# Two layers of a hybrid trunk: the S5 input projections on x times g, with the norm's scale put on behind them

## The chip, the core and the metric

The kernel runs on one core of one Trainium2 chip. A core has five engines, each with its own queue of instructions that it works off in order: PE multiplies matrices, DVE and ACT work on tiles, POOL and SP mostly issue transfers here. The metric is the device time of one execution in microseconds, lower is better.

## What is computed

The reference is a trunk of two layers on x of 512 positions by 1024 features, in float32. Cut to what matters:

```
def _rmsnorm(x, g):
    y = xf * lax.rsqrt(jnp.mean(xf * xf, axis=-1, keepdims=True) + RMS_EPS)
    return (y * g.astype(jnp.float32)).astype(x.dtype)
...
for i in range(DEPTH):                      # DEPTH = 2
    h = _rmsnorm(x, norm_mix_g[i])
    proj = h @ w_in[i]
    (z, xbc, dt_raw, q, k, v, qi, ki, wi, rwkv_cols, s5_u, gate_cols) = _split_last(proj, IN_SPLITS)
    ...                                     # four mixers: SSD, sparse attention, RWKV-7, S5
    x = x + (merged.astype(x.dtype) @ w_out[i]).astype(x.dtype)
    h = _rmsnorm(x, norm_ffn_g[i])
    x = x + _swiglu(h, ffn_w1[i], ffn_w3[i], ffn_w2[i]).astype(x.dtype)
return _rmsnorm(x, norm_final_g)
```

The norm divides every position by the root of its own mean square. The S5 mixer takes the 512 columns `s5_u` of the projection, and its state matrices come from small parameter tensors (`s5_a_re`, `s5_a_im`, `s5_log_dt`, `s5_b_*`, `s5_c_*`).

## The kernel before

x lies transposed, features on the partitions: eight tiles of 128 features by 512 positions. Each float32 operand of a large product is split in a rounded high part and a low part (`hh` and `hl` for h, `wh` and `wl` for weights), and a product takes three matmuls (`mm3`, L302 to L304: high by high, low by high, high by low). One projection of 128 columns (`pin`, through `proj`) is thus 8 times 3 = 24 matmuls of 128x512. Its weights come by one transfer of 512 KB on SP's queue into `raw` (two buffers); ACT rounds them to `wh` (L295), DVE subtracts to `wl` (L296). The output `pj` lies in one of two buffers in PSUM (`pp`): a projection starts only when the one two before it has been read out.

The code calls every piece of work with a class (`at("x0")`, `"w"`, `"e"`, `"m"`, `"x"`, `"u"`, in falling urgency), and a scheduler sorts the instructions of each engine by it once, at build time. On the chip nothing overtakes within an engine.

Start of layer 0. `first_stats` squares the four tiles of x as they come from memory (positions on the partitions), takes the root on ACT and scales x on DVE to `xs` (L210). `first_norm` turns `xs` by 32 transposes on PE (L221) and splits the result times g into `hh` and `hl` (L324, L325). `first_x` turns x itself by 32 more transposes (L231), copies it out (`xr`, L233) and stores it to `xd` in memory, for later. `s5_load` issues 13 transfers of S5 parameters on POOL's queue, in class `"w"`.

Start of layer 1. `norm` sums the squares over the features (`rstd`: 4 small products, L257, in 8 passes), spreads the reciprocal root over the partitions (`rep`: 4 products, L266), scales each tile to `h` (L281), rounds it (L282) and subtracts (L283).

Then, in both layers, `s5` calls four projections (u0 to u3 below) and ACT copies each from PSUM with its positions permuted (`us`, L968). In layer 0 DVE and ACT then build the S5 tables from the parameters: a chain of some 60 operations from `s5are` (L782) to `s5E` (L887), which ends in two steps for the first half of S5's groups, each followed by a group of 16 small matmuls (`s5_in`: 8 of L903, 8 of L904). In layer 1 these tables have been made during the feed-forward of layer 0. The next mixer, `dsa`, begins with a projection of 44 columns (`misc`), one for the index queries (QI) and then q, k and v. q takes the PSUM buffer that `misc` leaves when DVE has made `dskl` from it (L595).

The feed-forward's last loop runs over the eight output tiles d: 66 matmuls `pf`, then DVE adds them to x (L558), and ACT and DVE add the squares to `acc` (L249).

Of the kernel before, what the change touches and what calls it, by code (L numbers as in the profile page):

```python
# [10 lines left out]
F32 = mybir.dt.float32  # L11
# [74 lines left out]
class Trunk:  # L86
# [113 lines left out]
    def first_stats(self):  # L200
        nc = self.nc
        ss = self.sp.tile([128, 4], F32, name="ss", bufs=1)
        sr = self.sp.tile([128, 4], F32, name="sr", bufs=1)
        rr = self.sp.tile([128, 4], F32, name="rr", bufs=1)
        xs = [self.A(k, [D], f"xs{k}") for k in ("A0", "A1", "B5", "B6")]
# [5 lines left out]
        self.xs = xs  # L211

    def first_norm(self):
        nc = self.nc
        self.hh = self.cp.tile([128, KD, S], F32R, name="hh", tag="hh")
        self.hl = self.cp.tile([128, KD, S], F32R, name="hl", tag="hl")
# [8 lines left out]
    def first_x(self):  # L225
        nc = self.nc
        self.xd = self.dp.tile([D, S], F32, name="xd")
        for d in range(KD):
            ps = self.P("xrp")
            for t in range(4):  # L230
                nc.tensor.transpose(ps[:, t * 128:(t + 1) * 128], self.xt[t][:, d * 128:(d + 1) * 128], self.ident)  # L231
            x = self.T("xr")
            nc.scalar.copy(x, ps)  # L233
            self.q("xd").dma_start(self.xd[d * 128:(d + 1) * 128], x)
# [71 lines left out]
    def proj(self, pieces, M=128, act=None, mix=False):  # L306
# [8 lines left out]
    def pin(self, c0):  # L315
        return self.proj([(0, self.w_in[:, c0:c0 + 128])])
# [30 lines left out]
    def layer(self, i):  # L347
# [3 lines left out]
        if i == 0:  # L351
            with self.at("x0"):
                self.first_stats()
            with self.at("w"):
                self.s5_load(0, "B")
        with self.at("m", "Tb"):
            if i:
                self.norm("norm_mix_g")
            else:
                self.first_norm()  # L360
# [146 lines left out]
    def ffn(self):  # L507
# [1091 lines left out]
```

## Time and profile before

| | us |
|---|---|
| median of three runs | 2313.12 (2310.33 to 2317.92) |
| the profiled execution | 2318.86 |
| its span, on which all rows below count | 2317.1 |
| PE busy in the span | 2242.8 (97%) |
| DVE busy | 1448.4 (63%) |
| ACT busy | 921.0 (40%) |
| POOL busy | 103.6 (4%) |

The profile is of one execution. Rows of a timeline give the start in the span, the busy time, the engine, the line, what is written from what, how many instructions the row stands for and, in brackets, how long the engine had waited and for whom. Matmuls overlap, so that 24 of them take less than 24 times the busy time of one; from start to start is what counts.

### The profile page before, as it was taken

To read this page: it belongs to the slowest core of one execution; us is meant where nothing else is said; L and a number is where in the kernel's file an instruction comes from. 1 tells how busy PE (TensorE), PEld (TensorE's weight loads), DVE (VectorE), ACT (ScalarE), POOL (GpSimd) and SP (SyncE) were. 2 spreads that over 40 slices of the span, in tenths; PEclk is the share of its full clock that TensorE was granted. 3 is DMA by queue.
4 is the path that set the end of the run, shared out by engine and by line. 5 is a ranking of instruction groups with operands and counts; after the bars stand their busy time and mean duration, and the time that the engine had idled before them with its cause. 6 is when DMAs were issued, how large, how long until landed. Compare 5 with 4: busy or idle time off the path is not lost.

```text
span 2317.1 us, 32591 instructions
## 1 busy us (share of the span) xinstructions
PE 2242.8 (97%) x12660; PEld 1789.5 (77%) x12660; DVE 1448.4 (63%) x2676; ACT 921.0 (40%) x1455; POOL 103.6 (4%) x180
## 2 busy tenths in 40 slices
PE   6999999999999999999999999999999999999998
PEld 5777777777778888887878777687777888888786
DVE  5669867767678587543244696568668775444333
ACT  5443464244642343322233335533456333222232
POOL 3320000000000101000012000000000000000000
PEclk9999999999999999999999999999999999999999
DMA  7444552444166435433365445443333653333332
GB/s 219 114 104 128 144 170 80 116 101 124 55 205 204 119 92 166 125 97 105 111 187 150 123 124 168 123 101 105 91 110 106 222 160 91 100 97 95 89 98 86
DMA packets 429186, 290.08 MB, mean 125 GB/s; under 512 B 65024, under 2 KB 386768, under 8 KB 427432
## 3 DMA queue, kind: packets, MB, share of 16 engines
q1 hardware_dynamic: 419520, 261.45, 39.3%
q0 software_dynamic: 8512, 26.43, 4.1%
q8 instruction: 99, 1.62, 0.3%
q14 instruction: 55, 0.45, 0.1%
q10 hardware_dynamic: 1000, 0.13, 0.0%
HBM read 237.30 MB, written 51.43 MB: 125 GB/s over the span
## 4 chain that ended last, share of the span: by engine, by line
PE 81%; DVE 11%; DMA 4%; issue 2%; ACT 2%; SPq 0%; DVEq 0%; ACTq 0%; POOLq 0%
PE pj L303 16%; PE pj L304 16%; PE pj L302 16%; PE pf L304 3%; PE pf L302 3%; PE pf L303 3%; PE pb L302 3%; PE pb L303 3%; PE pb L304 3%; DVE wl L296 2%; DMA rnd<-rwrn 1%; PE lgp L656 1%; PE ptp L674 1%; PE po L679 1%; DVE score L709 1%
## 5 line engine op out<-in xcount | busy, mean ns | idle before, releaser
L302 PE MATMUL pj<-hh,wh 128*128 128x512 f32 x1888 | 750.1, 398 | 11.0 <-DVE conv L1453 4.9
L304 PE MATMUL pj<-hh,wl 128*128 128x512 f32 x1888 | 749.7, 397 | 0.4 <-DVE wl L296 0.4
L303 PE MATMUL pj<-hl,wh 128*128 128x512 f32 x1888 | 749.7, 397 | 0.1
L295 ACT CAST wh<-raw 128x1024 fp32r<-128x1024 f32 x336 | 348.6, 1037 | 922.6 <-PE pj L303 344.3
L296 DVE TENSOR_TENSOR wl<-raw,wh 128x1024 fp32r<-128x1024 f32 x336 | 405.2, 1206 | 350.8 <-ACT wh L295 348.9
L302 PEld LDWEIGHTS pj<-hh,wh 128*128 128x128 f32 x1888 | 356.3, 189 | 91.0 <-issue 8.6
L303 PEld LDWEIGHTS pj<-hl,wh 128*128 128x128 f32 x1888 | 356.4, 189 | 81.7 <-issue 9.0
L304 PEld LDWEIGHTS pj<-hh,wl 128*128 128x128 f32 x1888 | 356.0, 189 | 79.1 <-issue 6.3
L302 PE MATMUL pf<-hid,wh 128*128 128x512 f32 x352 | 137.9, 392 | 1.6 <-ACT wh L295 1.6
L304 PE MATMUL pf<-hid,wl 128*128 128x512 f32 x352 | 137.7, 392 | 0.5 <-DVE wl L296 0.5
L303 PE MATMUL pf<-hid,wh 128*128 128x512 f32 x352 | 136.9, 390 | 0.0
L302 PE MATMUL pb<-yh,wh 128*128 128x512 f32 x256 | 100.9, 394 | 0.0
L303 PE MATMUL pb<-yl,wh 128*128 128x512 f32 x256 | 100.8, 394 | 0.0
L304 PE MATMUL pb<-yh,wl 128*128 128x512 f32 x256 | 100.3, 392 | 0.0
L536 DVE TENSOR_TENSOR fa<-fa,pj 128x512 f32<-128x512 f32 x44 | 30.2, 688 | 95.3 <-PE pj L304 95.2
L533 DVE TENSOR_TENSOR fa<-pj,rb 128x512 f32<-128x512 f32 x44 | 30.4, 691 | 88.6 <-PE pj L304 88.6
L302 PEld LDWEIGHTS pf<-hid,wh 128*128 128x128 f32 x352 | 66.1, 188 | 16.8 <-ACT wh L295 3.4
L304 PEld LDWEIGHTS pf<-hid,wl 128*128 128x128 f32 x352 | 66.1, 188 | 16.0 <-DVE wl L296 2.6
L303 PEld LDWEIGHTS pf<-hid,wh 128*128 128x128 f32 x352 | 66.1, 188 | 13.4
L664 ACT ACTIVATE lg<-lg,mn 128x128 f32<-128x128 f32 (+3 forms) x64 | 35.8, 559 | 61.6 <-DVE mn L662 60.0
L302 PEld LDWEIGHTS pb<-yh,wh 128*128 128x128 f32 x256 | 48.1, 188 | 10.7 <-DVE m L476 0.7
L303 PEld LDWEIGHTS pb<-yl,wh 128*128 128x128 f32 x256 | 48.1, 188 | 9.8
(493 smaller groups left out, 2977.5 us busy)
## 6 DMA issues: line engine op xcount, KB each, us to landing
raw<-in_w_in SPq DMA_DIRECT2D x146, 512.0 KB
raw<-in_ffn_w SPq DMA_DIRECT2D x120, 512.0 KB
gates<-gate SPq DMA_DIRECT2D x64, 256.0 KB
gld<-gates SPq DMA_DIRECT2D x64, 256.0 KB
raw<-in_w_branch SPq DMA_DIRECT2D x32, 512.0 KB
raw<-in_w_out SPq DMA_DIRECT2D x16, 512.0 KB
raw<-in_ffn_w SPq DMA_DIRECT2D x16, 384.0 KB
bias<-relb POOLq DMA_DIRECT2D x16, 256.0 KB, 3.1
```

Of the source, the lines that this page charges most:

```text
L295: nc.scalar.copy(wh[:, :n], raw[:, :n])
L296: nc.vector.tensor_sub(wl[:, :n], raw[:, :n], wh[:, :n].bitcast(F32))
L302: mm(ps, wh, ah, start=first, stop=False)
L303: mm(ps, wh, al, start=False, stop=False)
L304: mm(ps, wl, ah, start=False, stop=last)
L533: nc.vector.tensor_mul(a, p1, rb)
L536: nc.vector.tensor_mul(a, a, p3)
L656: i = mm(ps[e][:, :W], q[er[e], qt * 128:(qt + 1) * 128], k[er[e], :W], start=True, stop=True)
L664: nc.scalar.activation(t[:, :W], t[:, :W], AF.Exp, scale=-1.0, bias=mn[e][:, qt:qt + 1], accum_out=sm[e][:, qt:qt + 1])
L674: nc.tensor.transpose(pp[:, b * 128:(b + 1) * 128], t[:, b * 128:(b + 1) * 128], self.ident)
L679: i = mm(po[er[e], qt * 128:(qt + 1) * 128], vt[:, b, er[e]], pt[:, e, b * 128:(b + 1) * 128], start=(b == 0), stop=(b == qt))
L709: nc.vector.match_replace(sc[:, :W], m8, sc[:, :W], PICK)
```

## The change

In both layers u0 to u3 are now projected from x times g, without the norm's factor. The factor r (one number per position) is put on when DVE reads u0 to u3 out of PSUM (`u_out`, a product with `rb`). Halfway in u1 the factor is spread over the partitions (`spread`, called as `mid`), and ACT copies it to `rb`. `rescale` then makes the h of the norm from x, g and `rb`, tile by tile, over the old `hh` and `hl`; of its eight subtractions four go to POOL. Everything from `misc` on uses these.

In layer 0 x is turned once, straight from the loaded tiles: ACT writes `hh` and half of the copies `self.x`, DVE the other half and `hl`; the stores to `xd` read `self.x`. The S5 loads wait, behind a copy of one column of the first weight tile (`late`). In layer 1 `hh` and `hl` of x times g are written inside the feed-forward's last loop, and `norm` is gone.

```diff
 def first_stats(self):
-            nc.scalar.activation(xs[t], self.xt[t], AF.Square, accum_out=ss[:, t:t + 1])
-            nc.scalar.activation(sr[:, t:t + 1], ss[:, t:t + 1], AF.Sqrt, scale=1.0 / D, bias=self.eps[:, 0:1])
-            nc.vector.reciprocal(rr[:, t:t + 1], sr[:, t:t + 1])
-            nc.vector.tensor_scalar(xs[t], self.xt[t], rr[:, t:t + 1], None, op0=OP.mult)
+            nc.scalar.activation(junk[:, t % 2], self.xt[t], AF.Square, accum_out=ss[:, t:t + 1])
+        nc.scalar.activation(sr, ss, AF.Sqrt, scale=1.0 / D, bias=self.eps[:, 0:1])
+        nc.vector.reciprocal(self.rr, sr)
...
+    def first_x(self):
         for d in range(KD):
             with self.at("x0", "TaTb"[d % 2 * 2:][:2]):
                 ps = self.P("xtp")
                 for t in range(4):
-                    nc.tensor.transpose(ps[:, t * 128:(t + 1) * 128], self.xs[t][:, d * 128:(d + 1) * 128],
+                    nc.tensor.transpose(ps[:, t * 128:(t + 1) * 128], self.xt[t][:, d * 128:(d + 1) * 128],
                                         self.ident)
-                self.split_out(self.hh[:, d], self.hl[:, d], ps, self.g0[:, d:d + 1])
+                g = self.g0[:, d:d + 1]
+                nc.scalar.activation(self.hh[:, d], ps, AF.Copy, scale=g)
+                eng = nc.vector.tensor_copy if d % 2 else nc.scalar.copy
+                eng(self.x[d], ps)
+                nc.vector.scalar_tensor_tensor(self.hl[:, d], self.x[d], g, self.hh[:, d].bitcast(F32),
+                                               op0=OP.mult, op1=OP.subtract)
...
-    def norm(self, g):
-        pr = self.rep(self.rstd(self.acc, 1.0 / D, self.eps[:, 0:1], "nrm"), "nrm")
+    def rescale(self, g, rb):
         for d in range(KD):
             h = self.T("h")
-            nc.vector.scalar_tensor_tensor(h, self.x[d], self.v(g, d), pr, op0=OP.mult, op1=OP.mult)
+            nc.vector.scalar_tensor_tensor(h, self.x[d], self.v(g, d), rb, op0=OP.mult, op1=OP.mult)
             nc.scalar.copy(self.hh[:, d], h)
-            nc.vector.tensor_sub(self.hl[:, d], h, self.hh[:, d].bitcast(F32))
+            eng = nc.gpsimd if d % 2 else nc.vector
+            eng.tensor_sub(self.hl[:, d], h, self.hh[:, d].bitcast(F32))
...
 # proj, over the 8 blocks k
+                if mid and k == KD // 2:
+                    mid()
...
 # feed-forward, last loop
                 nc.vector.tensor_add(self.x[d], self.x[d], ps)
                 if i < L - 1:
+                    self.split_out(self.hh[:, d], self.hl[:, d], self.x[d], self.v("norm_mix_g", d))
...
 def s5(self, ar):
-        for j in range(4):
-            ps = self.pin(C_U + j * 128)
-            us = self.T("us", tag="G")
-            nc.scalar.copy(us.rearrange("p (t c) -> p c t", c=64), ps.rearrange("p (c t) -> p c t", t=8))
+        def u_out(j, ps):
+            us = self.T("us", tag="G")
+            ct = lambda a: a.rearrange("p (c t) -> p c t", t=8)
+            tt(us.rearrange("p (t c) -> p c t", c=64), ct(ps), ct(rb), op=OP.mult)
...
+        pu = [self.pin(C_U)]
+        if not ahead:
+            with self.at("w"):
+                late = self.sp.tile([128, 1], F32, name="late", bufs=1)
+                self.s5_load(0, ar, after=nc.gpsimd.tensor_copy(late, self.raw[:, :1]))
+        with self.at("u"):
+            st = self.rstd(self.acc, 1.0 / D, self.eps[:, 0:1], "nrm") if ahead else self.rr
+        pu.append(self.pin(C_U + 128, spread))
+        with self.at("e"):
+            rb = self.T("rb", tag="KS")
+            nc.scalar.copy(rb, pr[0])
+        for j in range(4):
+            if j > 1:
+                pu.append(self.pin(C_U + j * 128))
+            with self.at("e"):
+                u_out(j, pu[j])
+        self.rescale("norm_mix_g", rb)
```

What this does to the sorted queues is shown at three places. The lines of the new code have moved by one or two: L301 to L303 are the three matmuls now.

PE in layer 0, at the first `s5kt` (L903), the first matmul that needs a finished `s5E` from DVE. Rows with 44 columns are `misc`, those with 128x512 QI. Before:

```order
L304 MATMUL pj<-hh,wl 44x512
L302 MATMUL pj<-hh,wh 128x512 [waits Activation_49]
L303 MATMUL pj<-hl,wh 128x512
L903 MATMUL s5kt<-s5tab_552,s5E 128x16 [waits DVE_49]
L904 MATMUL s5pt<-cst,s5E 128x128
```

After, the last rows of QI and what follows:

```order
L303 MATMUL pj<-hh,wl 128x512
L301 MATMUL pj<-hh,wh 128x512
L302 MATMUL pj<-hl,wh 128x512
L303 MATMUL pj<-hh,wl 128x512
L903 MATMUL s5kt<-s5tab_535,s5E 128x16 [waits DVE_49]
L904 MATMUL s5pt<-cst,s5E 128x128
```

Of QI two matmuls stood ahead of the first group of `s5kt`, and the second group stood between others of QI. Now all 24 stand ahead of it, both groups follow one another, and q comes behind both.

DVE in layer 0, from the second `us` on, ahead of the larger part of the S5 chain. Before, at the comparable place (L839 to L863 belong to the chain):

```order
L839 TENSOR_TENSOR s5erk<-s5erk,ere 128x32 [waits DVE_49]
L820 TENSOR_TENSOR s5t_534<-s5ami,s5are 128x32 [waits DVE_49]
L860 TENSOR_TENSOR s5tab<-s5raw,s5fr 128x512 [waits DMASW6_49,DMASW0_49]
L822 TENSOR_TENSOR s5t_534<-s5t_535,s5t_534 128x32 [waits DVE_49]
L839 TENSOR_TENSOR s5erk<-s5erk,ere 128x32
L296 TENSOR_TENSOR wl<-raw,wh 128x1024 [waits DMAHW1_49,PE_49,Activation_49]
```

After:

```order
L974 TENSOR_TENSOR us<-pj,rb 128x64x8 [waits PE_49]
L295 TENSOR_TENSOR wl<-raw,wh 128x352 [waits DMAHW5_49,DMAHW4_49,Activation_49]
L282 TENSOR_TENSOR hl<-h,hh 128x512 [waits Activation_49]
L279 SCALAR_TENSOR_TENSOR h<-x_107,cols,rb 128x512 [waits DVE_49]
L282 TENSOR_TENSOR hl<-h,hh 128x512 [waits Activation_49]
L279 SCALAR_TENSOR_TENSOR h<-x_107,cols,rb 128x512 [waits DVE_49]
L282 TENSOR_TENSOR hl<-h,hh 128x512 [waits Activation_49]
L279 SCALAR_TENSOR_TENSOR h<-x_107,cols,rb 128x512 [waits Pool_49]
L279 SCALAR_TENSOR_TENSOR h<-x_107,cols,rb 128x512 [waits DVE_49]
L974 TENSOR_TENSOR us<-pj,rb 128x64x8 [waits DMAHW6_49,PE_49]
```

All four `us`, eight `h` and DVE's four `hl` stand ahead of most of the chain; one `h` waits for POOL.

PE between the layers, from the last `pf` of the feed-forward. Before:

```order
L304 MATMUL pf<-hid,wl 128x512
L257 MATMUL nrms<-cst,acc 128x1 [waits DVE_49,PE_49]
L257 MATMUL nrms<-cst,acc 128x1 x3
L266 MATMUL nrmr<-cst,nrmst_9788 128x128 [waits DVE_49,PE_49]
L266 MATMUL nrmr<-cst,nrmst_9788 128x128 x3
L302 MATMUL pj<-hh,wh 128x512 [waits Activation_49]
```

After, the last block of u0 and the first of u1, 21 matmuls behind the last `pf`:

```order
L301 MATMUL pj<-hh,wh 128x512 [waits Activation_49]
L302 MATMUL pj<-hl,wh 128x512 [waits DVE_49]
L303 MATMUL pj<-hh,wl 128x512
L258 MATMUL nrms<-cst,acc 128x1 [waits DVE_49,PE_49]
L258 MATMUL nrms<-cst,acc 128x1 x3
L301 MATMUL pj<-hh,wh 128x512
```

The statistics' products have moved from ahead of u0 to behind it, and `nrmr` to the middle of u1.

## Rows read from the trace of the kernel before

**Rows 1.** the page, busy time of each engine, its share and instructions

```profile
PE 2242.8 (97%) x12660; PEld 1789.5 (77%) x12660; DVE 1448.4 (63%) x2676; ACT 921.0 (40%) x1455; POOL 103.6 (4%) x180
```

**Rows 2.** waits, 0 to 80 us: engine, line, released by; us, times, longest

```profile
PE pj L302 <- ACT us L968: 2.5, 1, 2.5
```

**Rows 3.** timeline of PE, layer 0: start, us, instruction, [idle before <- releaser]

```profile
20.06 0.50 PE L302 MATMUL pj<-hh,wh 128*128 128x512 f32 x1 [0.57 <-ACT hh L324]
...
63.88 0.40 PE L903 MATMUL s5kt<-s5tab,s5E 128*128 128x16 f32 x2 [1.53 <-DVE s5E L887]
...
66.51 0.63 PE L302 MATMUL pj<-hh,wh 128*128 128x512 f32 x1
...
69.50 0.59 PE L303 MATMUL pj<-hl,wh 128*128 128x512 f32 x1
...
75.79 0.40 PE L302 MATMUL pj<-hh,wh 128*128 128x512 f32 x1
```

**Rows 4.** timeline of DVE, the S5 chain of layer 0

```profile
30.81 0.19 DVE L782 COPY s5are<-s5ap 128x32 f32<-128x32 f32 x1 [3.73 <-PE s5ap L780]
...
44.46 0.19 DVE L805 TENSOR_TENSOR s5sh<-s5sh 128x32 f32<-128x32 f32 x1 [6.51 <-ACT s5sh L804]
...
62.59 1.24 DVE L887 TENSOR_TENSOR s5E<-s5E,s5tab 128x1024 f32<-128x1024 f32 x1
...
67.80 1.24 DVE L887 TENSOR_TENSOR s5E<-s5E,s5tab 128x1024 f32<-128x1024 f32 x1
```

**Rows 5.** groups by line, 0 to 80 us: ACT copies; DVE out of PSUM

```profile
L233 ACT COPY xr<-xrp 128x512 f32<-128x512 f32 x8 | 4.5, 591 | 6.9 <-DMA xd<-xr 6.9
...
L968 ACT COPY us<-pj 128x512 f32<-128x512 f32 x4 | 4.3, 1074 | 0.0
...
L322 DVE TENSOR_TENSOR dsql<-pj,dsqh 128x512 fp32r<-128x512 f32 x1 | 0.7, 683 | 0.0
```

**Rows 6.** timeline of POOL and ACT, the first 30 us

```profile
2.32 1.01 POOL L753 DMA_DIRECT2D s5raw<-in_s_a_re  x2
...
12.81 1.16 POOL L764 DMA_DIRECT2D s5raw<-in_s_c_im  x1
...
16.58 0.54 POOL L176 MEMSET sm<- 128x512 f32 x1
...
28.90 4.22 POOL L198 DMA_DIRECT2D relb<-rel  x8 [1.56 <-DMA rel<-oh]
...
9.21 1.06 ACT L207 ACTIVATE xsB<-xin 128x1024 f32<-128x1024 f32 x1 [0.18 <-DMA xin<-in_x]
...
18.37 1.04 ACT L295 CAST wh<-raw 128x1024 fp32r<-128x1024 f32 x1 [7.68 <-DMA raw<-in_w_in]
```

**Rows 7.** windows: stretch, length, busy of each engine (count), clock, DMA share, GB/s

```profile
0.00:10.00 10.00, 0.00 (x0) 0.00 (x0) 0.39 (x3) 6.49 (x12) 8.02 (x14) 1.00 0.83 268
```

**Rows 8.** timeline of PE, from layer 0 to layer 1

```profile
1172.80 0.39 PE L304 MATMUL pf<-hid,wl 128*128 128x512 f32 x1
...
1176.05 1.84 PE L257 MATMUL nrms<-cst,acc 128*128 128x1 f32 x8 [2.86 <-DVE acc L249]
...
1182.08 1.22 PE L302 MATMUL pj<-hh,wh 128*128 128x512 f32 x2 [1.49 <-ACT hh L282]
...
1212.04 0.39 PE L302 MATMUL pj<-hh,wh 128*128 128x512 f32 x1
```

**Rows 9.** timeline of DVE, same place: scaling h and its low part

```profile
1180.63 2.06 DVE L281 SCALAR_TENSOR_TENSOR h<-x,cols,nrmr 128x512 f32<-128x512 f32 x3 [2.23 <-PE nrmr L266]
...
1182.61 1.89 DVE L283 TENSOR_TENSOR hl<-h,hh 128x512 fp32r<-128x512 f32 x3
```

**Rows 10.** timeline of PE in the feed-forward of layer 0: statistics inside a projection

```profile
803.95 0.95 PE L257 MATMUL nrms<-cst,acc 128*128 128x1 f32 x8
...
804.76 0.49 PE L302 MATMUL pj<-hh,wh 128*128 128x512 f32 x1
...
810.34 1.05 PE L266 MATMUL nrmr<-cst,nrmst 128*128 128x128 f32 x8
```

More of the change, by code (lines that the diff above doesn't have):

```diff
@@ L220, in first_norm, with first_store, new_h @@
                 for t in range(4):
-                    nc.tensor.transpose(ps[:, t * 128:(t + 1) * 128], self.xs[t][:, d * 128:(d + 1) * 128],
+                    nc.tensor.transpose(ps[:, t * 128:(t + 1) * 128], self.xt[t][:, d * 128:(d + 1) * 128],
                                         self.ident)
-                self.split_out(self.hh[:, d], self.hl[:, d], ps, self.g0[:, d:d + 1])
-    def first_x(self):
-        nc = self.nc
-        self.xd = self.dp.tile([D, S], F32, name="xd")
-        for d in range(KD):
[L229 to L234, printed above, removed]
+                g = self.g0[:, d:d + 1]
[4 more added lines that the diff above has]
+                                               op0=OP.mult, op1=OP.subtract)
+    def first_store(self):
+        for d in range(KD):
+            self.q("xd").dma_start(self.xd[d * 128:(d + 1) * 128], self.x[d])
+    def new_h(self):
+        self.hh = self.cp.tile([128, KD, S], F32R, name="hh", tag="hh")
+        self.hl = self.cp.tile([128, KD, S], F32R, name="hl", tag="hl")
     def new_x(self):
@@ L288, in wload @@
         with self.at("w"):
-            raw = self.wp.tile([128, 1024], F32, name="raw", bufs=RAW)
+            raw = self.raw = self.wp.tile([128, 1024], F32, name="raw", bufs=RAW)
             wh = self.wp.tile([128, 1024], F32R, name="wh")
@@ L304, in mm3, with proj @@
         mm(ps, wl, ah, start=False, stop=last)
-    def proj(self, pieces, M=128, act=None, mix=False):
+    def proj(self, pieces, M=128, act=None, mix=False, mid=None):
         ah, al = act or ([self.hh[:, k] for k in range(KD)], [self.hl[:, k] for k in range(KD)])
@@ L351, in layer @@
         if i == 0:
+            self.first_x()
             with self.at("x0"):
                 self.first_stats()
[L354 to L360, printed above, removed]
+            with self.at("m", "Tb"):
                 self.load_cols(i)
                 self.set_cols()
-        if i == 0:
             with self.at("x", "Ta"):
                 self.rel_setup()
-                self.first_x()
+                self.first_store()
         self.gates = self.dp.tile([4 * KD, 128, S], F32, name="gates")
         self.gate_done = 0
-        self.dbg_out("h", lambda d: (self.hh[:, d].bitcast(F32), self.hl[:, d].bitcast(F32)))
         y = [None] * 4
@@ L518, in ffn @@
                     self.s5_ahead(i + 1, f)
+                    if f == 14:
+                        self.load_cols(i + 1)
             p1 = self.proj([(0, w1[:, f * 128:(f + 1) * 128])])
@@ L540, in ffn @@
         if i < L - 1:
-            with self.at("x", "Tb"):
-                self.load_cols(i + 1)
+            self.new_h()
         for d in range(KD):
@@ L545, in ffn @@
                 ps = self.P("pf")
-            if d == 1 and i < L - 1:
+            if d == 0 and i < L - 1:
                 with self.at("u", "Tb"):
@@ L743, in exp_acc, with s5_load, load @@
         return e, m1
-    def s5_load(self, i, ar, sl="24"):
+    def s5_load(self, i, ar, sl="24", after=None):
         I = self.I
+        def load(dst, src):
+            self.behind(self.q("sp").dma_start(dst, src), after)
         raw = self.A(ar + sl[0], [4, S], "s5raw")
@@ L752, in s5_load @@
             for r in range(2):
-                self.q("sp").dma_start(rows[:, j, r * 64:(r + 1) * 64], I[nm][i])
-        self.q("sp").dma_start(ldt, ap_of(I["s5_log_dt"][i], 0, [[0, 128], [1, 32]]))
+                load(rows[:, j, r * 64:(r + 1) * 64], I[nm][i])
+        load(ldt, ap_of(I["s5_log_dt"][i], 0, [[0, 128], [1, 32]]))
         B2, Bs = (raw[:, j].rearrange("p (g j) -> p g j", j=16) for j in range(2))
```

32 lines of the change are left out of this document (16 added, 16 removed).

## The prediction

> **What bounds the kernel now.** I read the page first: PE is busy for 2242.8 of 2317.1 us [rows 1]. So an edit counts by what it adds to PE's queue and by what PE waits for. Then the waits of the first 80 us, where layer 0 opens: there PE stands still 2.5 us because ACT has not read out a projection [rows 2]. Then the timelines of PE, where I mark three moments of layer 0. Its first projection starts at 20.06. Behind two matmuls of QI PE waits 1.53 us for `s5E`, and the first group of small matmuls runs at 63.88. The last projection before the mixers' own work, q, starts at 75.79 [rows 3]. The timeline of DVE shows who sets the second moment: DVE begins the S5 chain at 30.81, waits 6.51 us for ACT (which stood 6.9 us behind the stores of `xr`), and ends the first `s5E` at 62.59 + 1.24 = 63.83 [rows 4, 5]. Last, the change of layers: from the last `pf` at 1172.80 PE reaches QI at 1212.04, 39.2 us later [rows 8].
>
> I measure both places by the same yardstick, the start of q in layer 0 and of QI in layer 1. Behind them the queues are nearly the same in both kernels.
>
> **Change of layers.** Between the last `pf` and QI stand five projections (u0 to u3, `misc`). The 24 matmuls of one take 5.58 us where nothing is in the way (804.76 to 810.34) [rows 10]. Five take 27.9. The other 11.3 us are idle time (2.86, 1.49 and less), statistics at 1.84 and as much again, and matmuls at a slow spacing [rows 8]. After the change u0 needs only x times g, which is made block by block inside the loop: only its last block waits for the last x, 21 matmuls (4.8 us) behind. On that path lie an addition, a rounding and a subtraction, 0.6 to 0.7 us each by the rows of such tiles [rows 5, 9], 2.1 at most, so it is hidden. The statistics cost what they cost inside a busy stretch, 804.76 - 803.95 = 0.81, and 1.05 for the spreading [rows 10]. Sum: 0.2 for the last `pf`, 27.9 and 1.9: 30.0. Against 39.2 that is a gain of **9.2 us**. What could take from it: u2 needs the PSUM buffer of u0, which now waits for `rb`. `rb` is there about 0.6 us after the spreading, 3 us before u2 begins, and one `us` and a weight's `wl` fit in between. POOL's four subtractions can make `misc` late by 2 us. I allow 5 to 10.
>
> **Layer 0, the first projection.** ACT now does four squares, eight `hh` and four copies of x before the first weight tile. Twelve tiles at 0.59 [rows 5] are 7.1 us. The last tile of x is there at 9.21, when ACT takes it up [rows 6]; with the square at 1.06 and the transposes ahead, ACT comes to the weight at about 18.4, and its rounding ends at 19.4. Before, the weights themselves came at 18.37 [rows 6]. So u0 starts at about 20, as now: a wait for data has become a wait for ACT. The 32 transposes of x that stood among u0 to u2 are gone (3.5 us of PE), but u0 also no longer waits for splits.
>
> **Layer 0, the S5 loads.** The 13 loads occupied POOL from 2.32 to 13.97 [rows 6]. They now start behind the first weight tile, which without them lands at 12 to 15 (by the sizes of its tiles 2.9 MB have to come by then, and the core moved 268 GB/s over the first 10 us [rows 7]). The last are then issued at 24 to 27 and land, some 6 us later, at 30 to 33. PE meets their first reader in mid-u1, at 20 + 5.5 + 2.7 + 1.3 for the bias table's two products = 29.5. I take 29.5, with up to 3 us more.
>
> **Layer 0, the chain.** Before, DVE spent 63.83 - 30.81 = 33.0 us on it, 7.0 idle (6.51 and a 0.49): 26.0 of work. The stall behind `xr` goes, since nothing reuses the tiles of x. Some 0.9 of small work moves ahead, and one more `wl` (1.1) falls into it. Added ahead of it are:
> - four `us`. No row shows DVE writing with that permutation. Plain, from PSUM, it takes 0.68; ACT's permuted copy takes 1074 against 591 ns, 1.82 times as long [rows 5], which gives 1.24 as the other end. I take 0.95, the middle, since it is not seen that DVE pays for it: 3.8, between 2.7 and 5.0.
> - eight `h` at 2.06 / 3 = 0.69 and four `hl` at 1.89 / 3 = 0.63 [rows 9]: 5.5 + 2.5.
>
> Sum 26.0 - 0.9 + 1.1 + 3.8 + 5.5 + 2.5 = 38.0, and 1.5 of waiting for ACT's table and sines: 39.5. From 29.7 the first `s5E` is done at **69.2**. PE, which is free of that, runs half of u1, u2, u3, `misc` and QI: 29.5 + 2.0 for spreading and S5's small products + 2.8 + 4 x 5.5 + 0.4 = 56.7. There it stops, for 12.5 us. It has nothing else, because q takes the buffer of `misc`, which is freed behind `s5E` on DVE. The second `s5E` follows 4.1 us after the first (67.80 + 1.24 - 63.83, less the `wl` in between that is gone), and its group takes 2.2: q at 75.5. The clock: after its 1.53 us of idling PE ran seven matmuls from 66.51 to 69.50, 0.43 each in place of 0.23 [rows 3], a loss of 1.4; after a longer stop I take 2.5. POOL's subtractions: one `h` and then the chain wait for POOL. No row shows POOL on such a tile. Its nearest is a fill of 0.54 [rows 6], DVE's own 0.63. POOL comes to them only behind the S5 loads and the eight of the bias table (4.22) [rows 6], at about 31 to 38, while DVE asks for the first result at about 42. So the wait is between 0 and 4, and I take 1.5. Sum: 75.5 + 2.5 + 1.5 = 79.5 against 75.79: **3.7 us lost**, between 3 gained (short `us`, no POOL wait, loads early) and 11 lost.
>
> [...]
>
> **The rivals.**
> - *The chain is shorter than I sum it.* For it: two of my allowances, the permuted write and POOL, rest on no row. With `us` at 0.68, no wait on POOL and the clock back after 1.4 us, q starts at 75.5 - 1.1 + 1.4 = 75.8, and layer 0 costs nothing. Gain 9.2: about 2303.9. Against it: five waits of DVE for others are new here.
> - *POOL holds the chain.* If a subtraction on POOL takes twice DVE's (1.24, the time of DVE's 1024 columns [rows 4]) and DVE stands meanwhile, four cost 5 us in place of 1.5. Layer 0 loses 3.7 + 3.5 = 7.2, and 2.0 of the gain is left: 2311.1. [...]
> - *The S5 loads are late, and the kernel is slower.* PE itself stands in mid-u1 until the last load lands, for it reads C there. If the first weight tile lands as late as now, at 18.4, the loads are issued until 30 and land at 36 or later, and POOL reaches its subtractions only after 41 and four more. PE then stops 6 to 7 us in mid-u1, and DVE's chain starts that much later and meets POOL too (5). Layer 0 loses 3.7 + 6.5 + 3.5 = 13.7, and with a gain of 6 between the layers, where POOL cuts in too, the kernel is 7.7 slower: 2320.8. It decides from a landing of about 18 on. Against it: the loads themselves made up much of the traffic ahead of that tile.
> - *u0 of layer 1 is not free.* If u2 there waits 3 us for `rb` and `misc` 2 for POOL, the gain there is 4.2 and 0.5 is left: 2312.6.
>
> **How the numbers follow.** My sum is -9.2 + 3.7 = -5.5. The profiled execution took 2318.86, by 5.7 more than the median; its sum would be 2313.4. I subtract from the median: 2313.12 - 5.5 = **2307.6**. A measurement of this kernel can tell about 0.3% (6.9 us) from no change, which sets the bounds at 2306.2 and 2320.1. My forecast lies just inside. Chances: forecast 0.34, shorter chain 0.34, POOL 0.14, late loads 0.11, u0 not free 0.07. The first rival is faster; of the forecast's own spread a seventh (0.05) is too; the late loads are slower in nearly all. That gives faster 0.39, same 0.51, slower 0.10. The range runs from 2300 (the chain short and a gain of 10, with a gained start in layer 0) to 2318 (short of the worst landing).
>
> **What would show it.** Right: between the last `pf` of layer 0 and QI of layer 1 no idle time over 1 us and no slow spacing, 29 to 30 us in all; in layer 0 the largest wait of PE is `s5kt` for `s5E`, 10 to 15 us, and q starts at 78 to 81. Wrong: a wait of PE in mid-u1 for an S5 load; a wait of DVE's `h` or chain for POOL of more than 3 us; `us` rows beyond 1.2 us; PE idle before u2 or `misc` in layer 1; or q started before 76.

## The result and the profile after

The changed kernel takes 2327.64 us (median of 4 runs, 2325.03 to 2330.64). The kernel before took 2313.28 on the same chip, so the ratio is 1.0065 with a 95% interval of 1.0051 to 1.0079: **slower by 14.4 us**. I had forecast 2307.6. The profiled execution of after lasted 2325.68 (span 2323.9), 2.0 below its median; that of before lay 5.7 above its own. The two traces therefore differ by 6.8 us only.

The stages of the two traces say where. I cut the program at marks of PE: the first transpose of the attention (`ptp`), the first and the last product of the branches (`pb`) and of the feed-forward (`pf`) in each layer, and `mtp`, which stands just behind the reach of the change in layer 1. Lengths in us:

| stretch | before | after |
|---|---|---|
| start to the first `ptp` of layer 0 | 192.4 | 206.1 |
| to the first `pb` | 458.8 | 460.7 |
| `pb` | 103.6 | 103.6 |
| to the first `pf` | 291.9 | 291.9 |
| `pf` of layer 0 | 126.1 | 126.1 |
| last `pf` to `mtp` of layer 1 | 41.0 | 38.0 |
| to the first `pb` | 576.2 | 570.3 |
| `pb`, to the first `pf`, `pf` of layer 1 | 513.9 | 514.0 |
| to the end | 13.2 | 13.2 |

Four stretches (`pb` and `pf` of layer 0, the one between them, and the one from `pb` to `pf` in layer 1) agree within 0.2 us in every kernel that follows here. The two stretches of the mixers scatter: 452 to 461 us in layer 0 and 569 to 576 in layer 1, in kernels whose order there is the same. Before's profiled execution holds the longest of the second. By these two traces the change did two things: the opening of layer 0 (+13.7) and the change of layers (-3.0), together +10.7. The rest up to 14.4, that is 3.7 us, is smaller than that scatter, and no row that I found accounts for it. The time of before isn't the same each time either: measured beside the experiments below, it is 2308.99 to 2310.28, which is 3.0 to 4.3 us less than beside after. Against those, after loses about 18, and what the two openings leave unexplained is up to 7 us.

The page of after, busy time of each engine, and the clock of PE in 40 slices [rows 1]:

```profile
PE 2241.3 (96%) x12636; PEld 1789.6 (77%) x12636; DVE 1476.9 (64%) x2697; ACT 919.7 (40%) x1456; POOL 115.1 (5%) x189
...
PEclk9799999999999999999999999999999999999999
```

PE works as long as before (2241.3 against 2242.8), so the time is in waits. DVE has 28.5 us more to do. The waits of PE in after, 0 to 90 us (line, released by; us, times, longest) [rows 2]:

```profile
PE s5kt L903 <- DVE s5E L887: 11.9, 1, 11.9
PE xtp L220 <- DMA cst<-in_cst: 10.3, 1, 10.3
PE pj L302 <- DVE hl L282: 3.3, 1, 3.3
PE colp L438 <- DMA rows<-in_norm_final_g: 2.3, 1, 2.3
```

The largest is new. PE's timeline in layer 0 of after (start, us, instruction, idle before) [rows 3]:

```profile
19.22 0.80 PE L301 MATMUL pj<-hh,wh 128*128 128x512 f32 x1 [1.59 <-ACT wh L294]
...
25.17 0.61 PE L303 MATMUL pj<-hh,wl 128*128 128x512 f32 x1
...
29.89 0.31 PE L438 MATMUL colp<-cst,rows 108*128 108x108 f32 x1 [2.28 <-DMA rows<-in_norm_final_g]
...
57.41 0.66 PE L302 MATMUL pj<-hl,wh 128*44 128x512 f32 x1 [3.35 <-DVE hl L282]
...
79.42 0.61 PE L903 MATMUL s5kt<-s5tab,s5E 128*128 128x16 f32 x2 [11.94 <-DVE s5E L887]
...
87.97 0.77 PE L301 MATMUL pj<-hh,wh 128*128 128x512 f32 x1
```

The last row is the start of q, 12.2 us later than before (75.79). The row at 57.41 is a wait that I had not allowed for: `misc` waits for a low part `hl`. Now the S5 chain on DVE in after, and POOL beside it [rows 4]:

```profile
34.28 0.19 DVE L782 COPY s5are<-s5ap 128x32 f32<-128x32 f32 x1 [0.97 <-PE s5ap L780]
...
46.54 1.68 DVE L279 SCALAR_TENSOR_TENSOR h<-x,cols,rb 128x512 f32<-128x512 f32 x1
48.14 1.77 DVE L282 TENSOR_TENSOR hl<-h,hh 128x512 fp32r<-128x512 f32 x1
...
78.15 1.22 DVE L887 TENSOR_TENSOR s5E<-s5E,s5tab 128x1024 f32<-128x1024 f32 x1
```

```profile
46.38 2.98 POOL L282 TENSOR_TENSOR hl<-h,hh 128x512 fp32r<-128x512 f32 x2 [10.39 <-ACT hh L280]
51.49 1.63 POOL L282 TENSOR_TENSOR hl<-h,hh 128x512 fp32r<-128x512 f32 x1 [2.13 <-ACT hh L280]
54.46 2.35 POOL L282 TENSOR_TENSOR hl<-h,hh 128x512 fp32r<-128x512 f32 x1 [1.34 <-ACT hh L280]
```

The chain starts at 34.28 (30.81 before) and its first `s5E` ends at 78.15 + 1.22 = 79.37 (63.83 before): 45.1 us long against 33.0. While POOL subtracts, from 46.38 on, an `h` and an `hl` on DVE take 1.68 and 1.77, more than twice the 0.69 and 0.63 of [rows 9].

The change of layers in after, PE [rows 8]:

```profile
1188.45 0.39 PE L303 MATMUL pf<-hid,wl 128*128 128x512 f32 x1
1188.67 0.39 PE L301 MATMUL pj<-hh,wh 128*128 128x512 f32 x1
...
1194.11 0.95 PE L258 MATMUL nrms<-cst,acc 128*128 128x1 f32 x8
...
1199.90 1.13 PE L267 MATMUL nrmr<-cst,nrmst 128*128 128x128 f32 x8 [1.96 <-DVE nrmst L261]
...
1222.30 0.43 PE L302 MATMUL pj<-hl,wh 128*44 128x512 f32 x1 [2.80 <-DVE hl L282]
...
1223.49 0.43 PE L301 MATMUL pj<-hh,wh 128*128 128x512 f32 x1
```

u0 follows the last `pf` without a gap, as meant. But two waits are new, 1.96 and 2.80, and QI starts 35.0 us after the last `pf`, where I had 30.0 (39.2 before). Two fences show what stood behind them, first on ACT, then on DVE and POOL:

```profile
1197.37 1.05 ACT L294 CAST wh<-raw 128x1024 fp32r<-128x1024 f32 x1 [6.52 <-DMA raw<-in_w_in]
1198.32 0.26 ACT L260 ACTIVATE nrmst<-nrms,eps 128x4 f32<-128x4 f32 x1
```

```profile
1219.37 1.21 DVE L295 TENSOR_TENSOR wl<-raw,wh 128x1024 fp32r<-128x1024 f32 x1
1220.50 1.74 DVE L282 TENSOR_TENSOR hl<-h,hh 128x512 fp32r<-128x512 f32 x1
1220.34 1.35 POOL L282 TENSOR_TENSOR hl<-h,hh 128x512 fp32r<-128x512 f32 x1
```

The sums are there at 1194.11 + 0.95, but the square root stands in ACT's queue behind a rounding that waits for its weight until 1197.37. And `misc` waits until 1222.30 for the `hl` that ends last. That is DVE's, at 1220.50 + 1.74 = 1222.24 (POOL's ends at 1221.69). It stands behind a `us` and a weight's `wl`, and it takes 1.74 beside POOL's subtraction.

### The profile page after: what moved, and what is told of

It reads as the page before. It is cut to its first block, busy times and chain, and to the rows that moved or that the text cites. A ratio compares the mean times of both kernels' runs of the same rounds, so it can differ in the third digit from the quotient of the medians.

```text
span 2323.9 us, 32579 instructions
## 1 busy us (share of the span) xinstructions
PE 2241.3 (96%) x12636; PEld 1789.6 (77%) x12636; DVE 1476.9 (64%) x2697; ACT 919.7 (40%) x1456; POOL 115.1 (5%) x189
## 3 DMA queue, kind: packets, MB, share of 16 engines
q1 hardware_dynamic: 419520, 261.45, 39.3%
## 5 line engine op out<-in xcount | busy, mean ns | idle before, releaser
L301 PE MATMUL pj<-hh,wh 128*128 128x512 f32 x1888 | 749.7, 397 | 5.3 <-DVE conv L1476 3.7
L303 PE MATMUL pj<-hh,wl 128*128 128x512 f32 x1888 | 748.5, 397 | 0.0
L301 PEld LDWEIGHTS pj<-hh,wh 128*128 128x128 f32 x1888 | 356.5, 189 | 84.7 <-issue 6.4
L303 PEld LDWEIGHTS pj<-hh,wl 128*128 128x128 f32 x1888 | 355.9, 189 | 77.9 <-issue 6.0
L301 PE MATMUL pf<-hid,wh 128*128 128x512 f32 x352 | 137.9, 392 | 1.6 <-ACT wh L294 1.6
L303 PE MATMUL pf<-hid,wl 128*128 128x512 f32 x352 | 137.6, 392 | 0.5 <-DVE wl L295 0.5
L301 PE MATMUL pb<-yh,wh 128*128 128x512 f32 x256 | 100.9, 394 | 0.0
L303 PE MATMUL pb<-yh,wl 128*128 128x512 f32 x256 | 100.2, 392 | 0.0
L301 PEld LDWEIGHTS pf<-hid,wh 128*128 128x128 f32 x352 | 66.1, 188 | 16.8 <-ACT wh L294 3.4
L303 PEld LDWEIGHTS pf<-hid,wl 128*128 128x128 f32 x352 | 66.1, 188 | 16.0 <-DVE wl L295 2.6
L301 PEld LDWEIGHTS pb<-yh,wh 128*128 128x128 f32 x256 | 48.1, 188 | 10.8 <-DVE m L470 0.7
L303 PEld LDWEIGHTS pb<-yh,wl 128*128 128x128 f32 x256 | 48.1, 188 | 10.0
```

What stands on the lines that cost most here:

```text
L301: mm(ps, wh, ah, start=first, stop=False)
L303: mm(ps, wl, ah, start=False, stop=last)
```

## Experiments

Each cut of a diff is against after, that of e1 against before, and the comments `# e..` are mine. Differences in time are against the kernel before on the same chip (median 2308.99 for e1 to e4, 2310.28 for e5 to e8, 2309.69 for e9 and e10). `s5are`, `s5E`, q: start of the chain, end of the first `s5E`, start of q in layer 0. Change of layers: last `pf` to `mtp`, 41.0 before. After was timed beside the slower before, so that an experiment compares with after only to about 4 us.

| kernel | us | difference | ratio, 95% interval | `s5are` / `s5E` / q | change of layers |
|---|---|---|---|---|---|
| before | 2313.28 | | | 30.81 / 63.83 / 75.79 | 41.0 |
| after | 2327.64 | +14.4 | 1.0051 to 1.0079 | 34.28 / 79.37 / 87.97 | 38.0 |
| e1 layer 1 alone | 2310.55 | +1.6 | 0.9998 to 1.0021 | 30.65 | 36.8 |
| e2 e1, all on DVE | 2304.42 | -4.6 | 0.9971 to 0.9997 | 36.70 / 67.94 | 34.2 |
| e3 layer 0 alone | 2326.43 | +17.4 | 1.0070 to 1.0104 | 34.99 / 78.93 / 87.54 | 39.8 |
| e4 after, all on DVE | 2319.83 | +10.8 | 1.0034 to 1.0079 | 34.85 / 76.94 / 85.55 | 34.7 |
| e5 no rescaling | 2308.09 | -2.2 | 0.9982 to 1.0001 | 35.11 / 62.92 / 72.94 | 39.6 |
| e6 nor scaled `us` | 2303.17 | -7.1 | 0.9956 to 0.9980 | 36.41 / 61.07 / 69.70 | 39.3 |
| e7 loads early | 2325.90 | +15.6 | 1.0046 to 1.0087 | 34.54 / 78.43 / 87.04 | 38.2 |
| e8 PE kept busy | 2328.21 | +17.9 | 1.0059 to 1.0092 | 32.18 / 78.98 / 87.39 | 38.3 |
| e9 e2, later spread | 2303.46 | -6.2 | 0.9962 to 0.9985 | 30.69 | 34.3 |
| e10 rows on SP's queue | 2318.19 | +8.5 | 1.0023 to 1.0051 | 28.40 / 73.50 / 82.11 | 39.1 |

In e1, e2 and e9 the opening of layer 0 is before's; the starts in the table (30.65, 36.70, 30.69) show how far one order scatters.

**Which layer.** e1 keeps before's opening of layer 0, e3 before's change of layers.

```diff
+        ahead = i > 0
+        if not ahead:                 # e1: the loop of before
+            for j in range(4):
+                ps = self.pin(C_U + j * 128)
+                us = self.T("us", tag="G")
+                nc.scalar.copy(us.rearrange(...), ps.rearrange(...))
...
-                self.norm("norm_mix_g")
+            self.new_h()              # e1 keeps this of the change, e3 takes it back
```

> The opening of layer 0 is that of before (norm first, x turned twice, S5 loads at the start); only layer 1 opens as in the changed kernel. Theory: the loss is made in the opening of layer 0 (q there starts at 87.97 against 75.79), and the change of layers by itself gains (last pf to QI 35.0 us against 39.2). Then this kernel takes about 4 us less than before, 2309. Rival: the opening costs nothing of note and the loss of 14 us is spread over the mixers behind it, in both layers; then this kernel is slower than before, by 3 us or more.

> Layer 0 opens as in the changed kernel, layer 1 as before, with its norm ahead of the projections. Theory: all of the loss is here and nothing is gained between the layers: 12 us slower than before, 2325 to 2329, that is as slow as the changed kernel or slower by up to 4. Rival: layer 0 loses less than 8 us and the rest of the loss of the changed kernel comes from layer 1: under 2321.

e3 loses 17.4 us, so the loss is in layer 0. e1 did not gain the 4 us that I expected: its trace has the shorter change of layers (36.8 against 41.0), yet its median is not below before's. The two halves add up to 19.0 against the 14.4 of both, which their intervals (about 2.5, 4 and 3 us to each side) allow.

**POOL's half.** e2 is e1, and e4 is after, with all eight subtractions on DVE.

```diff
-            eng = nc.gpsimd if d % 2 else nc.vector
-            eng.tensor_sub(self.hl[:, d], h, self.hh[:, d].bitcast(F32))
+            nc.vector.tensor_sub(self.hl[:, d], h, self.hh[:, d].bitcast(F32))
```

> As e1, but the eight low parts of the rescaled h are all subtracted on DVE, none on POOL. Theory: in the changed kernel DVE's rows next to POOL's subtractions take 1.7 us in place of 0.7 because the two engines hold each other off, and misc waits 2.8 us for a low part; without POOL the DVE rows are 0.7, misc waits under 1 us, QI runs at full speed, and the time is 3 to 4 us under e1, about 2305.5. Rival: DVE has too much to do there and four more subtractions (2.5 us) make misc as late as POOL did; then e2 equals e1.

> The changed kernel with all subtractions of the rescaling on DVE in both layers. Theory (POOL and DVE hold each other off): in layer 0 the slow rows of h and hl lose 4.1 us and four subtractions add 2.5, so the first s5E comes 1.6 us earlier (from 79.4 to about 77.8) and q at about 86; with about 4 us between the layers the time falls by 5 to 6, to 2322. Rival (the rows are slow for another reason): rows of h and hl stay above 1.2 us, the first s5E comes 2.5 us later than in the changed kernel, and the time is 2328 to 2330.

DVE's groups between 36 and 60 us (operation, shape, count; busy us, mean ns; idle before), first after with POOL, then e4 without:

```profile
L279 DVE SCALAR_TENSOR_TENSOR h<-x,cols,rb 128x512 f32<-128x512 f32 x8 | 7.8, 991 | 0.1
L282 DVE TENSOR_TENSOR hl<-h,hh 128x512 fp32r<-128x512 f32 x4 | 4.9, 1224 | 0.0
L974 DVE TENSOR_TENSOR us<-pj,rb 128x512 f32<-128x512 f32 x4 | 4.3, 1076 | 0.2 <-PE pj L303 0.2
```

```profile
L279 DVE SCALAR_TENSOR_TENSOR h<-x,cols,rb 128x512 f32<-128x512 f32 x8 | 5.8, 741 | 0.0
L281 DVE TENSOR_TENSOR hl<-h,hh 128x512 fp32r<-128x512 f32 x8 | 5.3, 686 | 0.0
```

By the sums of their rows eight scalings and four subtractions cost DVE 12.7 us while POOL does the other four. Eight scalings and all eight subtractions cost it 11.1 without POOL. The help takes more from DVE than it gives. The chain of e4 is 42.1 us, 3.0 shorter. In time e2 is clearly faster than e1, with the same before beside both (-4.6 against +1.6). For e4 and after (10.8 against 14.4) the gain is less sure, with intervals of about 5 and 3 us in width, and it is under the 5 to 6 that I expected. POOL is the smaller part of the loss in layer 0: without it e4 still loses 10.8 us, and PE stops for 14.9, longer than in after because `misc` now waits for nothing ahead of it.

What one subtraction on POOL costs DVE is seen in e10 (below), where two small rows of the chain run beside it:

```profile
40.38 2.64 POOL L282 TENSOR_TENSOR hl<-h,hh 128x512 fp32r<-128x512 f32 x2 [7.90 <-ACT hh L280]
40.44 1.29 DVE L737 SCALAR_TENSOR_TENSOR erm<-erki,ere 128x32 f32<-128x32 f32 x1
41.77 1.31 DVE L738 TENSOR_TENSOR ere<-ere,erki 128x32 f32<-128x32 f32 x1
```

In after the same two rows, at 43.48 and 43.71, take 0.19 each, with POOL idle. So each is held for about 1.1 us, until a subtraction of POOL is done (DVE's rows end at 41.73 and 43.08; POOL's two, of 1.32 in the mean, end at 43.02). POOL itself needs 1.29 for one where DVE does nothing beside it (e1, at 1202.29).

**What in the chain.** e5 leaves out the rescaling in layer 0. e6 leaves out the factor on `us` as well, and ACT copies `us`.

```diff
-        self.rescale("norm_mix_g", rb)
+        if ahead:                     # e5 and e6
+            self.rescale("norm_mix_g", rb)
...
-            tt(us.rearrange("p (t c) -> p c t", c=64), ct(ps), ct(rb), op=OP.mult)
+            if ahead:                 # e6
+                tt(us.rearrange("p (t c) -> p c t", c=64), ct(ps), ct(rb), op=OP.mult)
+            else:
+                nc.scalar.copy(us.rearrange("p (t c) -> p c t", c=64), ct(ps))
```

> The changed kernel without the rescaling in layer 0: its projections behind the S5 ones work on x times g without the norm's factor, so eight products on DVE, eight roundings on ACT and eight subtractions are left out there; layer 1 is that of the changed kernel. Theory: the rescaling, put ahead of the S5 chain on DVE, makes the loss in layer 0. Its rows occupy 12 us of DVE there (37.7 to 57.3), so the first s5E comes at 67 to 68 in place of 79.4, misc waits for nothing, and the first transposes of the attention come at about 194 in place of 206: 2315, as before or 2 us off. Rival: the chain is late because the S5 loads and the first projection are; then s5E comes before 77 by little and the time stays above 2322.

> As e5, and in layer 0 the four S5 projections are copied out of PSUM by ACT without the factor, as before: the norm is left out of layer 0 altogether on DVE. Theory: each of the four products costs DVE 0.9 us, so s5E comes 3.6 us earlier than in e5, at about 64, where it came before the change (63.8), although the chain starts 3.4 us later; the attention's first transposes come at 191 to 192. Rival: PE's own work is the bound by then (QI ends at about 60 and the small groups and the clock follow), and e6 equals e5.

This takes the chain apart: 24.7 us in e6, 27.8 in e5, 45.1 in after. The four `us` cost 3.1, the rescaling 17.3, where I expected 12. The DVE groups of the two chains show what the 17.3 are: `h` and `hl` 12.7; one more `wl` (1.3) and one `s5xs` (1.2) that now fall ahead of `s5E`; 1.7 of idling; 0.4 are not assigned. Without it PE's stop is nearly gone (e5, PE):

```profile
62.97 0.40 PE L903 MATMUL s5kt<-s5tab,s5E 128*128 128x16 f32 x2 [0.96 <-DVE s5E L887]
...
68.65 0.61 PE L903 MATMUL s5kt<-s5tab,s5E 128*128 128x16 f32 x2 [3.13 <-DVE s5E L887]
...
72.94 0.77 PE L301 MATMUL pj<-hh,wh 128*128 128x512 f32 x1
```

q starts 15.0 earlier than in after, and the kernel is 16.6 us faster (-2.2 against +14.4). The mechanism that I had put first, DVE's chain with PE stopped behind it, is thereby shown.

**The place of the S5 loads.** e7 issues them at the start, as before did.

```diff
+            with self.at("w"):
+                self.s5_load(0, "B")          # in layer(), ahead of first_stats
...
-                late = self.sp.tile([128, 1], F32, name="late", bufs=1)
-                self.s5_load(0, ar, after=nc.gpsimd.tensor_copy(late, self.raw[:, :1]))
```

> The changed kernel with the S5 loads at the start of POOL's queue, as before, and without the copy of a weight's column. Theory: the place of the loads decides nothing: in the changed kernel PE did not wait for them in mid-u1, and s5ap started at 33.9 because u0 ran at the slow spacing and PE waited 2.3 us for the rows of colp; the time stays within 2 us of the changed kernel, 2326 to 2329. Rival: the loads made the opening late, and without the delay it falls to before's 30.8: 3 to 4 us less, 2323.5; or the small transfers delay x and the weights, and it is slower.

The sum does not change: +15.6, q at 87.04, `s5are` at 34.54. It is made of two effects that cancel. PE waits elsewhere with the loads early (its first transpose waits 13.9 for `cst` in place of 10.3, and the bias table's product 3.0 for its table), so that u0 starts at 23.38 and not at 19.22. But `colp` then waits for nothing.

**The clock in the gap.** e8 fills PE's stop with 44 products whose result nobody reads.

```diff
+        if self.i == 0:                       # behind split_out of QI
+            with self.at("u"):
+                ps = self.P("warm")
+                for n in range(44):
+                    mm(ps, self.hh[:, 1, :128], self.hh[:, n % KD], start=True, stop=True)
```

> The changed kernel with 44 products of 128x512 added on PE in layer 0 behind QI, where PE stands still for 11.9 us; their result is used by nothing. Theory: they end at about 77.5, before s5E, and PE's clock stays up: the two groups of s5kt and s5pt take 4.4 us in place of 8.5, but the second s5E ends at 83.4, so q starts at about 85.8 in place of 88.0 and at full speed: 3 to 3.5 us less than the changed kernel, 2324, although PE does 10 us more. Rival: the groups are slow for another reason, or the added products push s5kt back: as slow or slower by up to 2.

PE in e8 (in after the row at 79.42 answers to the second):

```profile
66.63 10.13 PE L615 MATMUL warm<-hh 128*128 128x512 f32 x44
79.03 0.40 PE L908 MATMUL s5kt<-s5tab,s5E 128*128 128x16 f32 x2 [2.26 <-DVE s5E L892]
...
83.10 0.61 PE L908 MATMUL s5kt<-s5tab,s5E 128*128 128x16 f32 x2 [1.47 <-DVE s5E L892]
...
87.39 0.77 PE L301 MATMUL pj<-hh,wh 128*128 128x512 f32 x1
```

The first group now runs in 2.3 us (79.03 to 81.3) in place of about 4.3. But the second must wait for the second `s5E` in any case, and by then the clock is down again (windows: length; busy and count of PE, PEld, DVE, ACT, POOL; granted clock; DMA share, GB/s):

```profile
77.00:83.00 6.00, 2.60 (x24) 2.37 (x24) 6.00 (x7) 2.98 (x4) 0.00 (x0) 0.87 0.01 2
83.00:88.00 5.00, 4.90 (x26) 4.81 (x27) 3.53 (x8) 2.85 (x6) 0.71 (x2) 0.50 0.07 15
```

q starts at 87.39, 0.6 earlier, and the time shows no gain (+17.9). The 3 to 3.5 us that I expected are not to be had this way.

**The start of the chain.** e10 moves the loads of parameter rows (18 in the opening) from ACT's queue to SP's.

```diff
-QUEUE = {"sp": "p", "qk": "a", "lc": "a", "sv": "a", "kt": "p", "bi": "p"}
+QUEUE = {"sp": "p", "qk": "a", "lc": "s", "sv": "a", "kt": "p", "bi": "p"}
```

> The changed kernel with the loads of the parameter rows (for colp) on SP's queue in place of ACT's, where they stood between the copies of x. Theory: PE's wait of 2.3 us for colp's rows goes and the S5 chain starts at about 32 in place of 34.3; the end of the chain, which sets q, follows by as much: q at about 86. Rival: SP's queue makes the weights late instead, u1 starts later and q stays at 88 or more.

It gave back 5.9 us, over twice what I expected (q at 82.11, the time +8.5 in place of +14.4; 9.5 by the times themselves). Two rows of ACT's timeline, the first weight's rounding in after and in e10, and two of PE in e10:

```profile
18.09 2.02 ACT L294 CAST wh<-raw 128x1024 fp32r<-128x1024 f32 x2
```

```profile
13.48 1.05 ACT L294 CAST wh<-raw 128x1024 fp32r<-128x1024 f32 x1
```

```profile
17.64 0.50 PE L301 MATMUL pj<-hh,wh 128*128 128x512 f32 x1
...
25.84 0.31 PE L438 MATMUL colp<-cst,rows 108*128 108x108 f32 x1 [0.59 <-DMA rows<-in_norm_final_g]
```

Three things come together in this kernel. With the loads gone from ACT's queue the planner also set the rounding 4.6 us earlier, between two `hh`, so u0 starts at 17.64 and not at 19.22, with no idle time ahead of it. It runs at 0.23 per product, not 0.43. And `colp` waits 0.59, not 2.28. That is 1.6, about 2.7 and 1.7 us by the rows. The run does not separate them.

The change had not made these loads late. The last load of a row leaves ACT's queue at the same moment in before and in after:

```profile
24.68 0.31 ACTq L434 DMA_DIRECT2D rows<-in_norm_final_g  x1
```

```profile
24.83 0.36 ACTq L428 DMA_DIRECT2D rows<-in_norm_final_g  x1
```

What is new is that PE comes to `colp` earlier: at 27.6 in after (29.89 - 2.28), at 30.28 and without a wait in before. In e10 the last of these loads leaves SP's queue at 21.62.

**The best of it.** e9 is e2 with the factor spread before the seventh block of u1, not the fifth.

```diff
-                if mid and k == KD // 2:
+                if mid and k == KD - 2:
```

> As e2 (layer 0 as before, layer 1 opens without the norm's factor, all subtractions on DVE), with the factor spread before the seventh of the eight blocks of u1 in place of the fifth, since in e2 PE waits 1.8 us there for the reciprocal root. Theory: this wait shrinks under 0.5 us, u2 still finds its buffer free or waits under 1 us, and the kernel is 5 to 7 us faster than before (ratio about 0.9975). Rival: the later factor makes u2 or misc wait by as much, and it equals e2 (ratio 0.9984).

PE's waits around the change of layers, first e2, then e9:

```profile
PE nrmr L271 <- DVE nrmst L265: 1.8, 1, 1.8
```

```profile
PE nrmr L271 <- DVE nrmst L265: 1.2, 1, 1.2
PE pj L304 <- DVE us L979: 0.5, 1, 0.5
```

The wait shrank by 0.6 and a 0.5 came up behind it, so the move itself is worth nothing (34.3 against 34.2). The time is the one that I expected, but not for the reason that I gave, a wait under 0.5: that is luck. Of the kernels that compute everything it is the fastest seen here, though e2's interval overlaps its own: 2303.46, a ratio of 0.9973 (0.9962 to 0.9985), faster than before by 6.2 us and than after by some 20 (20.6 by the differences, 24.2 by the times).

## Why the prediction was wrong

I forecast -5.5 and it was +14.4. Both halves of the sum failed, and both on the side of a loss: layer 0 lost 12.2 us up to q and not 3.7, the change of layers gave 4.2 up to QI and not 9.2. That is 8.5 and 5.0 of the 19.9 by which I missed. Another 1.5 was lost between q and the first `ptp` and 1.2 between QI and `mtp`, where I had held the queues to be the same and had not thought of the low clock that PE brings there (granted 0.69 from 88 to 92 us and 0.71 from 1222 to 1226 in after; in before 1.00 from 76 to 80 and from 1212 to 1216). The last 3.7 are the rest named above, for which I know no cause.

**Layer 0, the start: 4.6 us, the term that was missing.** I let the chain start at 29.7; it started at 34.28. u0 began at 19.22, near my 20. Behind that I took 5.5 us for u0 and no wait. In after its products run 0.43 apart until 25.6, about 3.0 us lost, and `colp` waits 2.28 for its rows; the 0.8 of the earlier start goes against that. The step that failed is that I let PE pass `colp` right behind u0. I had taken 32 transposes out of PE's queue ahead of it and did not ask when the loads that the change leaves where they are would be there. The last of them goes out at 24.83, as before (24.68), and PE now comes for it 2.7 us earlier. e10 takes the wait and the slow spacing away together; e8 agrees, whose chain starts at 32.18 with a wait of 1.09. What the last loads wait for in ACT's queue is not shown. The S5 loads, to which I gave a rival of their own, were in time: PE never waits for them, and in e7 their place changes nothing in the sum.

**Layer 0, the chain: 4.1 us, mis-sized in one term.** I had 38.0 + 1.5 for ACT + 1.5 for POOL = 41.0; it took 45.1. By e5 and e6 its parts were: base with the waits 24.7 (I had 27.7), `us` 3.1 (3.8), the rescaling 17.3 (5.5 + 2.5 + 1.5 = 9.5). The rescaling thus cost 7.8 more than I had; that the rest came out 3.7 cheaper, which hid nearly half of it, is luck. The permuted write, which I could not read from any row, was about right (1.08 busy and 0.92 from start to start, for my 0.95), and the step that failed is the one that I had taken from rows, `h` at 0.69 and `hl` at 0.63. Those rows [rows 9] come from a place where POOL does no arithmetic. Beside POOL the same tiles took 0.99 and 1.22 in the mean, 12.7 in all where I had 8.0; the `wl` and `s5xs` that fall into the chain and DVE's idling make up most of the rest.

POOL's part I had put at 1.5, from rows in which it touches no such tile. Beside its subtractions an `h` and an `hl` on DVE took 1.68 and 1.77 (after, at 46.54 and 48.14), against 741 and 686 ns in the mean without them (e4), and the small rows of e10 1.29 and 1.31 where they take 0.19 with POOL idle. e4's chain is only 3.0 shorter, but there DVE does the four subtractions itself, 2.7 us of work; against a helper that cost DVE nothing, POOL cost about 5.7. A subtraction on POOL took 1.61 in the mean of the eight of the run, 1.29 for the shortest and 2.35 for the longest, which ran from 54.46 on, beside a `wl` of DVE that took its 1.20. The first waited 10.39, until ACT's `hh` was there.

**Layer 0, the tail: right in length, in part by luck.** From the first `s5E` to q it took 8.6; I had 4.1 + 2.2 + 2.5 = 8.8. The stop of PE is 11.94 for my 12.5, at the place I named. But both of its ends came late by about as much: PE got there at 67.48 (79.42 - 11.94; I had 56.7), and `s5E` was done at 79.37 (69.2). PE's part in this is the late start, the 3.35 that `misc` waits and products 0.43 apart behind that wait, of which my sum had none. The loss to the clock is there: the granted clock is 0.50 from 79 to 88 us, behind a stop in which PE had 0.48 us of work in 12 (windows of after):

```profile
19.00:26.00 7.00, 6.78 (x16) 4.83 (x17) 6.62 (x21) 1.45 (x3) 4.19 (x6) 0.53 1.06 268
...
67.00:79.00 12.00, 0.48 (x3) 0.06 (x1) 11.05 (x15) 4.56 (x5) 0.00 (x0) 0.63 0.34 82
79.00:88.00 9.00, 8.58 (x49) 8.58 (x49) 7.36 (x9) 4.56 (x7) 0.50 (x1) 0.50 0.04 10
```

**Change of layers: 5.0 us too much.** u0 was free, as I said. The statistics were not: I took the 0.81 and 1.05 of a place [rows 10] where the square root is ready in time. Here it stood behind a weight's rounding in ACT's queue (1.96 us). `misc` waited 2.80 and 0.24 for DVE's `hl` beside POOL, where I allowed 2 as a risk and put nothing in the sum. After that wait QI's first products run 0.43 apart. With all subtractions on DVE (e2, e4) only the wait for the root is left, and 34.2 to 34.7 us to `mtp` against 38.0.

**Signs and rivals.** Of the signs that I set for being right, the place and length of PE's stop came true; q at 78 to 81 (87.97) and 29 to 30 us between the layers without a wait over 1 us (35.0, with two) did not. Of those for being wrong one came true, idle time ahead of `misc` in layer 1; there was no wait in mid-u1 for an S5 load. "POOL holds the chain" named a mechanism that was there, with a price of 5 against about 5.7 counted the same way, and with 2311.1 for a result. "The S5 loads are late" gave 2320.8, nearest to the time, and was wrong in its cause. The case that came true was none of the four: my own forecast's chain, with a late start in front of it, a rescaling nearly twice its price, and half of the gain between the layers. My range allowed 11 us of loss in layer 0 and 5 of gain between the layers each by itself, but its upper end (2318) did not take them together with a late start: 2313.1 + 11 - 5 is 2319 already.

Open are three things. What after loses beyond the two openings, 3.7 us or up to 7 by which before it is set against, has no cause that I can show; in the other kernels the like remainder lies between -3.4 and 6.7 us. The stretch from the first `ptp` to the first `pb` varies by 9 us among kernels with one order, so that I can't say whether the +1.9 of after belongs to the change. And e1's gain of 4.2 in the trace of the change of layers doesn't show in its median, whereas e2's does.

## What to carry to other kernels

Work that is taken off one engine's path lands in another engine's queue: before it is called hidden, ask which chain that queue feeds next, and count everything that will stand ahead of it, the start of that chain included. Here the same trick paid in layer 1, where DVE had room (e2, e9; in before it is busy for 18.2 of the 41.0 us from the last `pf` to `mtp`), and cost 17 us in layer 0, where DVE was already the engine that PE was about to wait for. Take the price of an operation from a row in which the same neighbours are at work, and where the change brings an engine to a place earlier, ask when the loads it needs there will land, also those that the change does not touch.

## What the runs showed of the hardware

- With POOL doing half of the subtractions DVE was busy longer than with none on POOL: 12.7 us for eight `h` and four `hl` beside POOL (after), 11.1 for eight and eight without it (e4). Two small rows of DVE that take 0.19 with POOL idle (after) took 1.29 and 1.31 beside its subtractions (e10); a subtraction takes POOL 1.29 where DVE does nothing beside it (e1).
- DVE reading a projection from PSUM and writing it permuted took 1.08 us per 128x512 tile (the four `us` of after), a plain one 0.68 [rows 5]; ACT's ratio was 1.82, DVE's was 1.6.
- u0 in layer 0 ran at half speed in after (0.43 per product; granted clock 0.53 from 19 to 26 us) after a wait of 1.59 us behind the transposes, and at 0.23 per product in e10, where nothing was waited for. The clock also differs between executions of one order: e1 and e2 have before's opening, and from 26 to 34 us it was 1.00 in before and e1, but 0.51 in e2.
- With PE kept busy for 10 us of its stop (e8) the granted clock was 0.87 from 77 to 83 us, and one group of small products ran in 2.3 us; after a further wait of 1.47 us the next ran at 0.50 (83 to 88 us).
